# Mixer input products by seven block products for eight, and all mixers ahead of projections and heads

## The chip, the cores and the metric

The kernel runs on one core of a Trainium2 chip. TensorE (PE) multiplies matrices into PSUM, VectorE (DVE) and GpSimd (POOL) do arithmetic on whole tiles, ScalarE (ACT) applies functions and copies, and SyncE (SP) issues most DMAs. Each engine works through its own instructions in order and waits on semaphores for the others. The metric is the time of one execution in microseconds (us): the median of the runs, with lowest and highest.

## The reference

The trunk has two layers over 2048 positions of width 1024. Cut to what matters:

```python
def _short_conv_mixer(h, w_in, w_conv, w_out):
    u = h @ w_in                                   # 1024 -> 4 * 1024
    b_gate, c_gate, xin, g = jnp.split(u, 4, axis=-1)
    y = b_gate * _causal_depthwise_conv(c_gate * xin, w_conv)      # width 3
    return (y * jax.nn.silu(g)) @ w_out

# layer 0:  x = x + mixer(rmsnorm(x));  k, v = split(rmsnorm(x) @ w_kv), 8 heads of 64
# layer 1:  q, g = split(rmsnorm(x) @ w_in_b)
#           z = q k^T / 8, strictly causal;  w = exp(z + reverse_cumsum(log_sigmoid(-z)))
#           x = x + ((w @ v) * silu(g)) @ w_out_b
# output:   rmsnorm(x)
```

So the products with `w_in` are about half of the dense work of both layers together: 1024 x 4096 weights for every position.

## The kernel before

**Tiles.** Everything is held transposed: features on the 128 partitions, positions along the tile. Positions are reversed and cut into four chunks of 512 columns; chunk 0 holds the earliest. A width of 1024 is 8 blocks of 128 (`KD`). Every fp32 operand of a dense product is split into a high and a low fp32r part (`split`, lines 477 to 479: ACT makes the high part, DVE the low part as a difference), and `mm3` (line 501) adds three products, high x high, high x low, low x high, for each of the 8 steps of k: 24 matmuls of 128 x 128 by 128 x 512 for one output block.

**Mixers.** `mixer_in` (line 573) takes chunks 0 and 1 together as part `m01`: for each of 8 column blocks `cb` it loads and splits the four weights C, X, B and G once, stores the split form to DRAM (`load_w`, line 487), and multiplies them with both chunks. Chunks 2 and 3 follow as parts `m2` and `m3`, which read the split weights back. For chunks 0 and 1 the RMS norm is applied late, to the products (`late_rms`, line 540); for chunks 2 and 3 the sums of squares come from `stats_x` (line 550) and the norm is applied to x in `norm_x` (line 558). After the products come p = C * X, the convolution with a halo of two columns carried from chunk to chunk, and the gates B and silu(G); the result goes to DRAM as `y_d`.

**The rest.** `fold_gains` (line 643) multiplies the norm gains into the weights of the heads and stores their split form. `proj_out` (line 667, parts `po0` to `po3`) computes the output projection of a chunk, its residual and norm. `proj` (line 737, `p00` to `p33`) makes k, q and v of two heads, `proj_gate` (line 742, `g0` to `g3`) the gates. `attention` (line 752, `a00` to `a37`: chunk and head) goes over blocks of 512 keys from the latest to the first; for each of four groups of 128 queries it takes a sigmoid of the scores, a running product on DVE (`tensor_tensor_scan`), and a multiplication, then transposes the weights on PE, splits them and multiplies them with v. Only the block on the diagonal is shortened. `out_b`, `out_norm`, `out_b_last` and `finish` (lines 841 to 920) are the last projection and norm.

**Order.** Nothing is issued while these functions run. A recorder (lines 168 to 350) keeps every operation, gives it a key from the table `PLAN` (start and end per part, line 32), and `order` then builds each engine's fixed order: at each step it takes, of all operations whose inputs and tile buffers are free by a table of costs, the one that can start first, and of those the one with the lowest key. Buffers have tags with a number of turns (line 24: `whl` for split weights, `wraw` for raw weights, `act` for split activations, `og`, `ld`, `w`, `R`, ...); a tile must wait until an earlier tile of its tag is done with. All recorded instructions are emitted at line 350, which is why the profile names that line for nearly all of them, and tiles are told apart by their names: `pC`, `pX`, `pB`, `pG` are the mixer's input products, `po` the output projection, `pk`, `pq`, `pv`, `pg` the heads' products, `z`, `R`, `w`, `wt`, `wth`, `wtl`, `av` those of attention, `pob` and `pol` the last projection.

Of the kernel before, what the change touches and what calls it, by code (L numbers as in the profile page):

```python
# [10 lines left out]
F32 = mybir.dt.float32  # L11
# [5 lines left out]
P = 128  # L17
# [6 lines left out]
NR, NW, NT, NL, NWB, NRAW, NA, NWTS = 5, 8, 4, 5, 4, 2, 16, 2  # L24
# [143 lines left out]
class Recorder:  # L168
# [76 lines left out]
    def places(self, plan):  # L245
# [15 lines left out]
        for o in self.ops:  # L261
            o.left = len(o.deps)
            for d in o.deps:
                d.after.append(o)

        todo, n = [o for o in self.ops if not o.left], 0
        while n < len(todo):
            o = todo[n]
            n += 1
            for u in o.after:  # L270
                u.key = max(u.key, o.key)
                u.left -= 1
                if not u.left:
                    todo.append(u)
        rank = {id(o): k for k, o in enumerate(todo)}
        done = sorted(self.ops, key=lambda o: (o.key, rank[id(o)]))
# [82 lines left out]
def kernel(  # L359
# [121 lines left out]
    def w_tile(nm, kt=KD):  # L481
# [504 lines left out]
```

## Time and profile before

| | |
|---|---|
| median of 3 runs | 1809.22 us (1808.72 to 1812.49) |
| profiled execution, its own time | 1809.78 us |
| its span | 1808.1 us, granted TensorE clock 0.99 |
| HBM read and written | 326.92 MB and 136.05 MB |

The span runs from the first to the last instruction of the profiled execution. The profile gives for each engine its busy time, for each group of instructions its count and duration, and for each idle time the instruction that ended it. PE is an exception: matmuls overlap in its pipeline and their ends are modelled, so a matmul's listed mean (0.39 us) is longer than the distance between two of them.

### The profile page before, as it was taken

What the parts mean: (1) busy time and instruction counts of PE and PEld (TensorE: products, weight loads), DVE (VectorE), ACT (ScalarE), POOL (GpSimd) and SP (SyncE); (2) the same over time, 40 slices, a digit from 0 to 9 for tenths busy, and PEclk for the clock granted to TensorE, in tenths of its full rate; (3) what the DMA queues carried; (4) which work ended last, traced back from release to release, by engine and by line L of the source; (5) the groups of instructions that cost most, each with busy time, mean ns of one, the idle gap of its engine ahead of it and who ended that gap; (6) DMA issues with size and microseconds to landing.
All of it is one profiled execution on the core that took longest, in us unless ns stands there. A gap on an engine that the chain in (4) does not pass through costs nothing.

```text
span 1808.1 us, 24782 instructions
## 1 busy us (share of the span) xinstructions
PE 1755.3 (97%) x8312; PEld 1425.4 (79%) x8312; DVE 1234.5 (68%) x1830; ACT 777.2 (43%) x1493; POOL 418.5 (23%) x814
## 2 busy tenths in 40 slices
PE   7999999999999999999999999999999999999994
PEld 5788888887888888888878878888887888787762
DVE  6876644464244363558386749997468999999995
ACT  5433311232133232335243436665345666677652
POOL 5100000101021021112021312333112223346464
PEclk9999999999999999999999999999999999999996
DMA  9999955699878798668666576555878656879886
GB/s 298 331 352 352 363 200 162 202 306 352 289 272 273 239 352 267 240 218 302 216 228 230 184 249 206 181 185 185 273 241 313 210 193 221 277 240 322 265 285 206
DMA packets 234639, 464.63 MB, mean 257 GB/s; under 512 B 18704, under 2 KB 125200, under 8 KB 209936
## 3 DMA queue, kind: packets, MB, share of 16 engines
q1 hardware_dynamic: 174432, 404.28, 64.9%
q10 hardware_dynamic: 59920, 58.74, 11.2%
q8 instruction: 66, 1.08, 0.2%
q14 instruction: 61, 0.50, 0.1%
q0 software_dynamic: 160, 0.02, 0.1%
HBM read 326.92 MB, written 136.05 MB: 256 GB/s over the span
## 4 chain that ended last, share of the span: by engine, by line
PE 79%; DVE 9%; DMA 6%; issue 4%; ACT 1%; POOL 1%; SPq 0%; ACTq 0%; POOLq 0%; DVEq 0%
PE pB L350 9%; PE pG L350 9%; PE pC L350 9%; PE po L350 8%; PE pX L350 8%; PE av L350 6%; PE z L350 6%; PE wt L350 5%; PE pk L350 5%; PE pv L350 4%; PE pq L350 4%; PE pg L350 3%; PE pob L350 3%; DVE R L350 3%; DVE w L350 2%
## 5 line engine op out<-in xcount | busy, mean ns | idle before, releaser
L350 DVE TENSOR_TENSOR_SCAN R<-R,R,ones 128x512 f32<-128x512 f32 x192 | 250.4, 1313 | 15.3 <-ACT R L350 14.9
L350 ACT ACTIVATE R<-z 128x512 f32<-128x512 f32 (+2 forms) x320 | 173.6, 544 | 150.3 <-PE z L350 114.0
L350 ACT CAST wth<-wt 128x512 fp32r<-128x512 f32 (+2 forms) x320 | 156.1, 526 | 178.7 <-PE wt L350 146.2
L350 DVE TENSOR_TENSOR wtl<-wt,wth 128x512 fp32r<-128x512 f32 (+2 forms) x320 | 181.8, 598 | 64.9 <-ACT wth L350 61.4
L350 PE MATMUL pC<-h,whl_C 128*128 128x512 f32 x768 | 207.0, 399 | 8.3 <-ACT whl_C L350 8.0
L350 PE MATMUL z<-kt,q 128*128 128x512 f32 (+2 forms) x640 | 207.8, 387 | 1.8 <-DMA kt<-k_d 1.0
L350 PE MATMUL pB<-h,whl_B 128*128 128x512 f32 x768 | 208.3, 395 | 1.1 <-ACT whl_B L350 1.0
L350 PE MATMUL pG<-h,whl_G 128*128 128x512 f32 x768 | 207.1, 395 | 0.0
L350 PE MATMUL po<-y,whl_o 128*128 128x512 f32 x768 | 205.0, 394 | 0.5 <-ACT y L350 0.5
L350 DVE TENSOR_TENSOR w<-w,R 128x512 f32<-128x512 f32 (+2 forms) x320 | 201.3, 642 | 5.4 <-POOL R L350 0.5
L350 PE MATMUL pX<-h,whl_X 128*128 128x512 f32 x768 | 201.3, 396 | 0.4 <-ACT whl_X L350 0.4
L350 PE MATMUL wt<-ident,w 128*128 128x128 f32 x1088 | 195.9, 274 | 3.6 <-DVE w L350 3.4
L350 ACT ACTIVATE w<-z 128x512 f32<-128x512 f32 (+2 forms) x320 | 171.8, 544 | 49.9 <-PE z L350 48.0
L350 PEld LDWEIGHTS pC<-h,whl_C 128*128 128x128 f32 x768 | 143.1, 190 | 41.1 <-ACT whl_C L350 8.0
L350 PEld LDWEIGHTS wt<-ident,w 128*128 128x128 f32 x1088 | 139.6, 140 | 44.4 <-DVE w L350 10.9
L350 POOL COPY R<-R 128x1 f32<-128x1 f32 x192 | 93.5, 487 | 325.3 <-DVE R L350 273.5
L350 PEld LDWEIGHTS pX<-h,whl_X 128*128 128x128 f32 x768 | 142.6, 188 | 32.6 <-issue 1.9
L350 PEld LDWEIGHTS po<-y,whl_o 128*128 128x128 f32 x768 | 142.7, 188 | 31.6 <-ACT y L350 0.9
L350 PEld LDWEIGHTS pB<-h,whl_B 128*128 128x128 f32 x768 | 141.8, 188 | 29.9 <-ACT whl_B L350 1.5
L350 PEld LDWEIGHTS pG<-h,whl_G 128*128 128x128 f32 x768 | 142.4, 188 | 28.4
L350 DVE TENSOR_TENSOR_SCAN R<-R,ones 128x128 f32<-128x128 f32 (+3 forms) x128 | 112.2, 885 | 40.8 <-POOL R L350 39.4
L350 PEld LDWEIGHTS z<-kt,q 128*128 128x128 f32 x640 | 112.3, 189 | 20.4 <-ACT w L350 1.8
(152 smaller groups left out, 2593.2 us busy)
## 6 DMA issues: line engine op xcount, KB each, us to landing
whl_o<-sw_o SPq DMA_DIRECT2D x24, 1024.0 KB, 6.1
kt<-k_d ACTq DMA_DIRECT2D x80, 256.0 KB, 4.2
vv<-v_d ACTq DMA_DIRECT2D x80, 256.0 KB, 4.8
whl_C<-sw_C SPq DMA_DIRECT2D x16, 1024.0 KB, 6.0
whl_X<-sw_X SPq DMA_DIRECT2D x16, 1024.0 KB, 6.4
whl_k<-sw_kv SPq DMA_DIRECT2D x16, 1024.0 KB, 7.1
whl_B<-sw_B SPq DMA_DIRECT2D x16, 1024.0 KB, 6.7
whl_G<-sw_G SPq DMA_DIRECT2D x16, 1024.0 KB, 5.7
```

Of the source, the lines that this page charges most:

```text
L350: getattr(o.engine.engine, o.name)(*map(real, o.args), **{k: real(v) for k, v in o.kw.items()})
```

## The change

**Seven products for eight.** Two gates form a pair, (C, X) and (B, G). For one column block, the two gates times the two halves of the input width are a 2 x 2 table of weight blocks, A; the two halves of the input times two chunks are a 2 x 2 table of operands, B. Each block product has 4 steps of k instead of 8, so the plain way is 8 block products of 12 matmuls. `fast_unit` takes 7, with sums of weight blocks (`s1` to `s4`) and of operands (`t1` to `t4`), and accumulates parts of them in three PSUM banks (`fa`, `fd`, `fe`). ACT copies a bank at three points (`keep`), DVE adds a bank to a copy at three.

**What feeds it.** `fast_weights` loads four raw blocks, forms the seven weights and splits them; in the first pair of chunks it also stores them, and the second pair reads them back. Column blocks 0 and 1 of chunks 0 and 1 stay plain (`NPL = 2`), so the second pair forms those two again. `fast_first` and `fast_rest` (parts `x0`, `x1`) build the 7 x 4 operands of chunks 0 and 1 from x and the late norm, with their sums on POOL; `fast_all` (part `x2`) builds those of chunks 2 and 3, with the sums on DVE. There is one set of operand buffers, under tags that attention uses later (`HOMES`).

**Order.** `m2` and `m3` are replaced by one part for each pair of chunks and column block (`m02` to `m07`, `m20` to `m27`). `PLAN` is new in all its numbers. The tiles of the output projection (`act`) come after the operands of the second pair, so all mixers come ahead of it. `places` now takes keys in the order of recording. Split weights are held as tiles of 4 steps of k (`Q`), so the output projection and the heads load two tiles for one. Nothing else in projections and attention changes.

```diff
-NR, NW, NT, NL, NWB, NRAW, NA, NWTS = 5, 8, 4, 5, 4, 2, 16, 2
+NR, NW, NT, NL, NWB, NRAW, NA, NWTS = 5, 8, 4, 5, 8, 4, 16, 2
+
+Q, NPL = 4, 2
...
-    "m01": (-696.3, -373.1), "s2": (116.9, 307.1), "s3": (-527.4, -474.4), "fold": (141.2, 142.2),
...
+    "m01": (-29.9, 8.6), "x0": (-61.5, 68.4), "x1": (10.0, 14.7), "s2": (58.9, 306.1), "s3": (218.5, 388.6),
...
+    def w_tile(nm, kt=Q):
...
+        first = key not in split_d
+        if first:
+            split_d[key] = [dram.tile([P, 2, Q, P], F32, name=f"sw_{nm}_{j}") for j in range(0, kt, Q)]
+        wts = []
+        for j, d in enumerate(split_d[key]):
+            wt = w_tile(f"{nm}_{j}")
+            if first:
+                raw = sb.tile([P, Q, P], F32, name=f"wr_{nm}_{j}", tag="wraw", bufs=NRAW)
+                nc.sync.dma_start(out=raw, in_=src[j * Q * P:(j + 1) * Q * P, :].rearrange("(k p) n -> p k n", p=P))
+                split(wt[:, 0], wt[:, 1], raw, eng)
+                nc.sync.dma_start(out=d, in_=wt.bitcast(F32))
+            else:
+                nc.sync.dma_start(out=wt.bitcast(F32), in_=d)
+            wts.append(wt)
+        return wts
...
-            tag, bufs = (("w", NW), ("R", NR) if k < NR else ("ld", NL))[c]
+            tag, bufs = (("og", KD), ("ld", NL) if k < NL else ("vv", 2) if k == NL else ("ot", 2))[c]
...
-        if len(cs) == 1:
-            h[cs[0]] = norm_x(cs[0])
-        for cb in range(KD):
+
+        for cb in range(NPL):
...
+    HOMES = {"b11": ["w"] * 8, "t1": ["R"] * 5 + ["wth"] * 2 + ["wtl"], "t2": ["act"] * 4, "b22": ["act"] * 4,
+             "b21": ["act"] * 4, "t3": ["act"] * 4, "t4": ["q2", "q2", "kt", "kt", "vv", "vv"]}
+    BUFS = {"w": NW, "R": NR, "wth": NWTS, "wtl": NWTS, "act": NA, "q2": 2, "kt": 2, "vv": 2}
+    fast_b = {}
+    def operand(c, nm, k, raw):
+        if k == 0:
+            fast_b[c, nm] = []
+            home[nm] = list(HOMES[nm])
+        tag = home[nm].pop(0)
+        if tag in ("act", "q2"):
+            t = sb.tile([P, 2, CH], F32R, name=f"op_{nm}_{c}_{k}", tag=tag, bufs=BUFS[tag])
+            pair = (t[:, 0, :], t[:, 1, :])
+        else:
+            tags = [tag, home[nm].pop(0)]
+            pair = tuple(sb.tile([P, CH], F32R, name=f"op{m}_{nm}_{c}_{k}", tag=tg, bufs=BUFS[tg]) for m, tg in enumerate(tags))
+        split(pair[0], pair[1], raw)
+        fast_b[c, nm].append(pair)
+    home = {}
+    def fast_norm(x, k, r):
+        nc.vector.scalar_tensor_tensor(out=x, in0=x, scalar=gains["a"][:, k:k + 1], in1=r, op0=ALU.mult, op1=ALU.mult)
+    def fast_first(c):
+        x1, x2 = x_in[c + 1], x_in[c]
+        for k in range(Q):
+            fast_norm(x1[k], k, late[c + 1][0])
+            fast_norm(x2[k], k, late[c][0])
+            operand(c, "b11", k, x1[k])
+            nc.gpsimd.tensor_sub(x1[k], x2[k], x1[k])
+            operand(c, "t1", k, x1[k])
+        for k in range(Q):
+            fast_norm(x2[k + Q], k + Q, late[c][0])
+            fast_norm(x1[k + Q], k + Q, late[c + 1][0])
+            nc.gpsimd.tensor_sub(x1[k], x2[k + Q], x1[k])
+            nc.gpsimd.tensor_sub(x2[k], x2[k + Q], x2[k])
+    def fast_rest(c):
+        x1, x2 = x_in[c + 1], x_in[c]
+        for k in range(Q):
+            operand(c, "t2", k, x1[k])
+            operand(c, "b22", k, x2[k + Q])
+            operand(c, "b21", k, x1[k + Q])
+            operand(c, "t3", k, x2[k])
+            nc.gpsimd.tensor_sub(x1[k + Q], x1[k + Q], x1[k])
+            operand(c, "t4", k, x1[k + Q])
+    def fast_all(c):
+        rs = []
+        for i in (c, c + 1):
+            r = sb.tile([P, CH], F32, name=f"rs_{i}", tag="acc", bufs=2)
+            nc.scalar.copy(r, bcast(rx[i], f"hb{i}"))
+            rs.append(r)
+        for k in range(Q):
+            b = {}
+            for nm, i, kk in (("b11", 1, k), ("b12", 0, k), ("b22", 0, k + Q), ("b21", 1, k + Q)):
+                x = b[nm] = sb.tile([P, CH], F32, name=f"x{nm}_{c}_{k}", tag="og", bufs=KD)
+                nc.sync.dma_start(out=x, in_=xT[kk * P:(kk + 1) * P, cols(c + i)])
+                fast_norm(x, kk, rs[i])
+            operand(c, "b11", k, b["b11"])
+            nc.vector.tensor_sub(b["b11"], b["b12"], b["b11"])
+            operand(c, "t1", k, b["b11"])
+            nc.vector.tensor_sub(b["b11"], b["b22"], b["b11"])
+            operand(c, "t2", k, b["b11"])
+            nc.vector.tensor_sub(b["b12"], b["b22"], b["b12"])
+            operand(c, "b22", k, b["b22"])
+            operand(c, "b21", k, b["b21"])
+            operand(c, "t3", k, b["b12"])
+            nc.vector.tensor_sub(b["b21"], b["b21"], b["b11"])
+            operand(c, "t4", k, b["b21"])
+    NAMES = ("a11", "s1", "s2", "s4", "a12", "s3", "a22")
+    def fast_weights(c, cb, gs):
+        nm = f"{gs[0][0]}{cb}_{c}"
+        key = ("fast", gs[0][0], cb)
+        w = {}
+        if key in split_d:
+            for n in NAMES:
+                w[n] = w_tile(f"{n}_{nm}")
+                nc.sync.dma_start(out=w[n].bitcast(F32), in_=split_d[key][n])
+            return w
+        if c == 0:
+            split_d[key] = {n: dram.tile([P, 2, Q, P], F32, name=f"sw_{n}_{nm}") for n in NAMES}
+        a = {}
+        for n, (g, i), j in (("a11", gs[0], 0), ("a21", gs[1], 0), ("a22", gs[1], Q), ("a12", gs[0], Q)):
+            a[n] = sb.tile([P, Q, P], F32, name=f"fr_{n}_{nm}", tag="wraw", bufs=NRAW)
+            src = w_in_a[0][j * P:(j + Q) * P, i * D + cb * P: i * D + (cb + 1) * P]
+            nc.sync.dma_start(out=a[n], in_=src.rearrange("(k p) n -> p k n", p=P))
+        def sp(n, raw):
+            w[n] = w_tile(f"{n}_{nm}")
+            split(w[n][:, 0], w[n][:, 1], raw)
+            if c == 0:
+                nc.sync.dma_start(out=split_d[key][n], in_=w[n].bitcast(F32))
+        sp("a11", a["a11"])
+        sp("a22", a["a22"])
+        nc.vector.tensor_add(a["a22"], a["a21"], a["a22"])
+        sp("s1", a["a22"])
+        nc.vector.tensor_sub(a["a21"], a["a11"], a["a21"])
+        sp("s3", a["a21"])
+        nc.vector.tensor_sub(a["a11"], a["a22"], a["a11"])
+        sp("s2", a["a11"])
+        sp("a12", a["a12"])
+        nc.vector.tensor_sub(a["a12"], a["a12"], a["a11"])
+        sp("s4", a["a12"])
+        return w
+    def fast_unit(c, cb, gs, w):
+        nm = f"{gs[0][0]}{cb}_{c}"
+        def product(bank, wn, bn, start, stop):
+            n = 0
+            for k in range(Q):
+                for i, m in ((0, 0), (0, 1), (1, 0)):
+                    nc.tensor.matmul(bank, w[wn][:, i, k, :], fast_b[c, bn][k][m], start=start and n == 0,
+                                     stop=stop and n == 3 * Q - 1, skip_group_check=True)
+                    n += 1
+        def keep(n, ps):
+            t = ld512(f"{n}_{nm}")
+            nc.scalar.copy(t, ps)
+            return t
+        a = psum.tile([P, CH], F32, name=f"fa_{nm}", tag="lin", bufs=NLIN)
+        d = psum.tile([P, CH], F32, name=f"fd_{nm}", tag="z", bufs=NZ)
+        e = psum.tile([P, CH], F32, name=f"fe_{nm}", tag="wt", bufs=NWT)
+        product(a, "a11", "b11", True, False)
+        c11 = keep("f1", a)
+        product(d, "s1", "t1", True, False)
+        p5 = keep("f5", d)
+        product(a, "s2", "t2", False, False)
+        c12 = keep("f2", a)
+        product(d, "s4", "b22", False, True)
+        nc.vector.tensor_add(c12, c12, d)
+        product(e, "a12", "b21", True, True)
+        nc.vector.tensor_add(c11, c11, e)
+        product(a, "s3", "t3", False, False)
+        nc.vector.tensor_add(p5, p5, a)
+        product(a, "a22", "t4", False, True)
+        return ((c12, p5), (c11, a))
+    conv = {}
+    def fast_conv(cb, c, cc, x):
+        p = sb.tile([P, CH + 2], F32, name=f"p_{cb}_{c}", tag="p", bufs=2)
+        nc.vector.tensor_mul(p[:, 0:CH], x, cc)
+        nc.gpsimd.tensor_copy(p[:, CH:CH + 2], halo[:, cb, :])
+        nc.gpsimd.tensor_copy(halo[:, cb, :], p[:, 0:2])
+        t = conv[cb, c] = t512(f"cv_{cb}_{c}")
+        nc.scalar.activation(t, p[:, 0:CH], AF.Copy, scale=cw[:, 2, cb:cb + 1])
+        nc.vector.scalar_tensor_tensor(out=t, in0=p[:, 1:CH + 1], scalar=cw[:, 1, cb:cb + 1], in1=t,
+                                       op0=ALU.mult, op1=ALU.add)
+        nc.vector.scalar_tensor_tensor(out=t, in0=p[:, 2:CH + 2], scalar=cw[:, 0, cb:cb + 1], in1=t,
+                                       op0=ALU.mult, op1=ALU.add)
+    def fast_out(cb, c, b, g):
+        t = conv[cb, c]
+        nc.vector.tensor_mul(t, t, b)
+        sg = t512(f"sg_{cb}_{c}")
+        nc.scalar.activation(sg, g, AF.Sigmoid)
+        nc.vector.tensor_mul(t, t, sg)
+        nc.vector.tensor_mul(t, t, g)
+        nc.sync.dma_start(out=y_d[c][cb], in_=t)
+    def mixer_fast(c, cb):
+        for gs, use in (((("C", 1), ("X", 2)), fast_conv), ((("B", 0), ("G", 3)), fast_out)):
+            w = fast_weights(c, cb, gs)
+            for i, (first, second) in enumerate(fast_unit(c, cb, gs, w)):
+                use(cb, c + i, first, second)
...
+    part("x0", fast_first, 0)
+    part("x1", fast_rest, 0)
     for c in (2, 3):
         part(f"s{c}", stats_x, c)
     part("fold", fold_gains)
-    for c in (2, 3):
-        part(f"m{c}", mixer_in, (c,))
+    part("x2", fast_all, 2)
+    for c in (0, 2):
+        for cb in range(NPL if c == 0 else 0, KD):
+            part(f"m{c}{cb}", mixer_fast, c, cb)
```

More of the change, by code (lines that the diff above doesn't have):

```diff
@@ L261, in places @@
         for o in self.ops:
-            o.left = len(o.deps)
             for d in o.deps:
                 d.after.append(o)
[L266 to L276, printed above, removed]
+                assert d.index < o.index
+                o.key = max(o.key, d.key)
+        done = sorted(self.ops, key=lambda o: (o.key, o.index))
         for k, o in enumerate(done):
@@ L465, in rstd_bcast, with square_into @@
         return bcast(rstd(acc, nm), nm)
-    def square_into(acc, src, first, nm, eng=nc.vector, early=False):
+    def square_into(acc, src, first, nm, eng=nc.vector, home=("t", NT)):
         if first:
@@ L470, in square_into @@
         else:
-            tag = "wth" if early else "t"
-            sq = sb.tile([P, CH], F32, name=f"sq_{nm}", tag=tag, bufs=NT if tag == "t" else NWTS)
+            sq = sb.tile([P, CH], F32, name=f"sq_{nm}", tag=home[0], bufs=home[1])
             nc.scalar.activation(sq, src, AF.Square)
@@ L487, in load_w @@
     def load_w(src, key, nm, kt=KD, eng=nc.vector):
-        if key not in split_d:
-            wt = w_tile(nm, kt)
-            raw = sb.tile([P, kt, P], F32, name=f"wr_{nm}", tag="wraw", bufs=NRAW)
-            nc.sync.dma_start(out=raw, in_=src.rearrange("(k p) n -> p k n", p=P))
-            split(wt[:, 0], wt[:, 1], raw, eng)
-            split_d[key] = dram.tile([P, 2, kt, P], F32, name=f"sw_{nm}")
-            nc.sync.dma_start(out=split_d[key], in_=wt.bitcast(F32))
-            return wt
-        wt = w_tile(nm, kt)
-        nc.sync.dma_start(out=wt.bitcast(F32), in_=split_d[key])
-        return wt
+        first = key not in split_d
[13 more added lines that the diff above has]
+        return wts
     def mm3(ps, wts, a, kt=KD):
-        hi, lo = wts[:, 0], wts[:, 1]
         n = 0
         for k in range(kt):
-            for w, m in ((hi, 0), (hi, 1), (lo, 0)):
-                nc.tensor.matmul(ps, w[:, k, :], a[k][:, m, :], start=n == 0, stop=n == 3 * kt - 1)
+            for w, m in ((0, 0), (0, 1), (1, 0)):
+                nc.tensor.matmul(ps, wts[k // Q][:, w, k % Q, :], a[k][:, m, :], start=n == 0, stop=n == 3 * kt - 1)
                 n += 1
@@ L536, in squares @@
         for k, x in enumerate(xs):
-            square_into(acc, x, k == 0, f"h{c}{k}", nc.gpsimd, early=True)
+            square_into(acc, x, k == 0, f"h{c}{k}", nc.gpsimd, ("wth", NWTS))
         return acc
@@ L541, in late_rms @@
         pb = bcast(y, f"h{c}")
-        r = sb.tile([P, CH], F32, name=f"rs_{c}", tag="w", bufs=NW)
+        r = sb.tile([P, CH], F32, name=f"rs_{c}", tag=("kt", "wtl")[c], bufs=2)
         nc.scalar.copy(r, pb)
-        r2 = sb.tile([P, CH], F32, name=f"rs2_{c}", tag="w", bufs=NW)
+        r2 = sb.tile([P, CH], F32, name=f"rs2_{c}", tag=("kt", "vv")[c], bufs=2)
         nc.scalar.activation(r2, pb, AF.Square)
@@ L553, in stats_x @@
         for k in range(KD):
-            square_into(acc, load_x(c, k, "s"), k == 0, f"h{c}{k}", early=True)
+            square_into(acc, load_x(c, k, "s"), k == 0, f"h{c}{k}")
         y = const.tile([P, 4], F32, name=f"rx_{c}")
         rx[c] = rstd(acc, f"h{c}", y)
-    def norm_x(c):
-        hc = []
-        pb = bcast(rx[c], f"hb{c}")
-        for k in range(KD):
-            x = load_x(c, k, "n")
-            nc.vector.scalar_tensor_tensor(out=x, in0=x, scalar=gains["a"][:, k:k + 1], in1=pb,
-                                           op0=ALU.mult, op1=ALU.mult)
-            hc.append(act_tile(f"h_{c}", k))
-            split(hc[k][:, 0, :], hc[k][:, 1, :], x)
-        return hc
     h = {}
     turn = [0]
-    late_acc, late = {}, {}
+    late_acc, late, x_in = {}, {}, {}
     def mixer_in(cs):
-        if len(cs) == 1:
-            h[cs[0]] = norm_x(cs[0])
-        for cb in range(KD):
+        for cb in range(NPL):
             wts = {}
@@ L646, in fold_gains @@
             for i in range(KD):
-                split_d[nm, i] = dram.tile([P, 2, KD, P], F32, name=f"sw_{nm}{i}")
+                split_d[nm, i] = [dram.tile([P, 2, Q, P], F32, name=f"sw_{nm}{i}_{j}") for j in range(0, KD, Q)]
                 for j in range(0, KD, 4):
@@ L662, in fold_gains @@
             for m, t in enumerate((hi, lo)):
-                nc.sync.dma_start(out=split_d["ob", ob][:, m], in_=t.bitcast(F32))
+                nc.sync.dma_start(out=split_d["ob", ob][0][:, m], in_=t.bitcast(F32))
     kept = {}
@@ L875, in out_b_last @@
         for ob in range(KD):
-            wts = w_tile(f"ob{c}_{ob}", 3)
-            nc.sync.dma_start(out=wts.bitcast(F32), in_=split_d["ob", ob][:, :, 0:3, :])
+            wts = [w_tile(f"ob{c}_{ob}", 3)]
+            nc.sync.dma_start(out=wts[0].bitcast(F32), in_=split_d["ob", ob][0][:, :, 0:3, :])
             ps = lin(f"pob_{c}_{ob}")
@@ L883, in out_b_last @@
         for ob in range(KD):
-            nc.sync.dma_start(out=wl[ob // 4][:, :, ob % 4, :].bitcast(F32), in_=split_d["ob", ob][:, :, 3, :])
+            nc.sync.dma_start(out=wl[ob // 4][:, :, ob % 4, :].bitcast(F32), in_=split_d["ob", ob][0][:, :, 3, :])
         sg = sb.tile([P, CH], F32, name=f"sgl_{c}", tag="hl", bufs=1)
```

18 lines of the change are left out of this document (8 added, 10 removed), and 37 rows, old and new, of the table PLAN.

## The prediction

> **What bounds the kernel now.** I read the page's engine totals first, then the slices, then the chain that ended last.
>
> ```profile
> span 1808.1 us, 24782 instructions
> PE 1755.3 (97%) x8312; PEld 1425.4 (79%) x8312; DVE 1234.5 (68%) x1830; ACT 777.2 (43%) x1493; POOL 418.5 (23%) x814
> ...
> PE   7999999999999999999999999999999999999994
> ...
> DVE  6876644464244363558386749997468999999995
> ...
> PE 79%; DVE 9%; DMA 6%; issue 4%; ACT 1%; POOL 1%; SPq 0%; ACTq 0%; POOLq 0%; DVEq 0%
> ```
>
> TensorE (PE) has work in every slice and carries 79% of the chain: it is the bound. VectorE (DVE) averages 68%, but its slices go from 2 to 9; the 9s lie at the end. What a PE saving is worth therefore depends on whether DVE can still feed PE afterwards. The stretches, with the columns of the view in its first line:
>
> ```profile
> core 0: us, PE busy (x) PEld busy (x) DVE busy (x) ACT busy (x) POOL busy (x), PEclk, DMA share, GB/s
> 0.00:107.00 107.00, 95.66 (x404) 74.85 (x405) 79.17 (x121) 54.11 (x84) 30.09 (x39) 1.00 1.02 322
> ...
> 0.00:370.00 370.00, 358.65 (x1571) 292.83 (x1571) 221.06 (x324) 126.53 (x185) 43.59 (x66) 1.00 0.87 284
> 370.00:1400.00 1030.00, 1021.82 (x4885) 835.64 (x4885) 639.56 (x979) 400.87 (x823) 204.25 (x488) 1.00 0.74 252
> ...
> 1400.00:1500.00 100.00, 100.00 (x524) 81.88 (x522) 97.21 (x135) 67.27 (x135) 24.04 (x61) 1.00 0.61 201
> ...
> 1600.00:1700.00 100.00, 97.70 (x485) 77.11 (x484) 97.01 (x129) 71.05 (x137) 49.53 (x71) 1.00 0.85 288
> ...
> 1750.00:1808.10 58.10, 28.83 (x109) 19.18 (x107) 36.52 (x61) 14.60 (x25) 31.54 (x24) 0.74 0.68 219
> ```
>
> To see: up to 370 us the plain products of chunks 0 and 1 run with PE full and DVE at 60%. From 370 to 1400 the products of chunks 2 and 3 stand between the heads, and DVE is at 62%. From 1400 on DVE is at 97%, and PE still loses only 0 to 2.3 us in 100. In the last 58 us both run dry.
>
> **What the change removes.** The four groups of input products, and two of them in order of time (the first column is the start):
>
> ```profile
> L350 PE MATMUL pC<-h,whl_C 128*128 128x512 f32 x768 | 207.0, 399 | 8.3 <-ACT whl_C L350 8.0
> ...
> L350 PE MATMUL pB<-h,whl_B 128*128 128x512 f32 x768 | 208.3, 395 | 1.1 <-ACT whl_B L350 1.0
> L350 PE MATMUL pG<-h,whl_G 128*128 128x512 f32 x768 | 207.1, 395 | 0.0
> ...
> L350 PE MATMUL pX<-h,whl_X 128*128 128x512 f32 x768 | 201.3, 396 | 0.4 <-ACT whl_X L350 0.4
> ```
>
> ```profile
> 101.77 5.60 PE L350 MATMUL pG<-h,whl_G 128*128 128x512 f32 x24
> 107.21 5.60 PE L350 MATMUL pC<-h,whl_C 128*128 128x512 f32 x24
> ```
>
> 24 matmuls take 107.21 - 101.77 = 5.44 us, so one costs 0.2267 us. A unit (one gate pair, one column block, two chunks) had 4 x 24 = 96 of them and now has 7 x 12 = 84. Chunks 0 and 1 have 2 x 6 such units (column blocks 0 and 1 stay plain), chunks 2 and 3 have 2 x 8: 28 units x 12 = 336 matmuls, **76.2 us** of PE. Nothing else leaves PE; the output projection, heads and attention keep their counts.
>
> **What it adds.** None of it on PE; prices from these groups (count, busy, mean ns of one):
>
> ```profile
> L350 DVE SCALAR_TENSOR_TENSOR cv<-p,cw,cv 128x512 f32<-128x512 f32 x64 | 47.7, 745 | 11.1 <-ACT cv L350 9.5 <-POOL p L350 0.9
> ...
> L350 DVE TENSOR_TENSOR x<-x,po 128x512 f32<-128x512 f32 x32 | 21.9, 686 | 70.8 <-PE po L350 70.8
> ...
> L350 ACT COPY cs<-pC 128x512 f32<-128x512 f32 x32 | 18.8, 588 | 66.8 <-PE pC L350 63.9 <-DMA vv<-v_d 2.8
> ...
> L350 DVE SCALAR_TENSOR_TENSOR cv<-p,cw,cv 128x512 f32<-128x512 f32 x64 | 47.7, 745 | 11.1 <-ACT cv L350 9.5 <-POOL p L350 0.9
> ...
> L350 DVE SCALAR_TENSOR_TENSOR xn<-xn,g_a,prb_hb 128x512 f32<-128x512 f32 x16 | 11.3, 736 | 2.3 <-PE prb_hb L350 2.3
> ...
> L350 DVE TENSOR_TENSOR fold_kv<-fold_kv,fold_kv 128x512 fp32r<-128x512 f32 x16 | 11.0, 686 | 1.4 <-ACT fold_kv L350 1.1
> ```
>
> A unit lasts 84 x 0.2267 = 19.0 us. Beside it run three ACT copies of 0.59 (1.8 us) and three DVE adds of 0.69 (2.1 us). Where its seven weight forms are made (12 units of chunks 0 and 1, 4 of chunks 2 and 3) come 7 splits and 4 sums, 11 x 0.69 = 7.6 us of DVE. Per column block of two units in the first pair, DVE has 2 x (7.6 + 2.1) + 4.4 for the two convolutions (0.69 + 2 x 0.745 each) + 6 x 0.69 for the gates = 27.9 us in 38.1: hidden, with 10.2 us to spare. Without that cover each instruction would cost PE its 0.69. In the second pair DVE has less still, so folding the gains (72 instructions of 0.69 us, 50 us) goes under it. ACT's work is under half of the unit. DMA: a column block of the first pair reads 2.1 MB and stores 14 forms of 0.52 MB and 0.5 MB of gates, 10 MB; at the 322 GB/s of the first row above that is 31 us, under 38.1, so it costs nothing while the queue keeps its lead, and a gain has no reason.
>
> *Start of the first pair.* The normed x (16 x 0.736 = 11.8), the 28 splits (19.2) and the first unit's weights (7.6) are 38.6 us of new DVE work; in the first 107 us, about the length of the plain part, DVE idles 107 - 79.2 = 27.8. Excess 10.8. The 16 POOL subtractions take 16 x 1.41 = 22.6 us more, and how far DVE can work beside them shows here:
>
> ```profile
> 1754.23 2.19 POOL L350 TENSOR_TENSOR acc_x<-acc_x,sq_x 128x512 f32<-128x512 f32 x1
> 1756.37 1.72 POOL L350 TENSOR_TENSOR x2r<-x2r,pbs 128x512 f32<-128x512 f32 x1
> ```
>
> ```profile
> 1755.27 3.36 DVE L350 TENSOR_TENSOR w<-w,R 128x512 f32<-128x512 f32 x2
> ```
>
> Two DVE products took 3.36 us instead of 1.4 beside two POOL ones. Without any overlap the excess is 10.8 + 22.6 = 33.4. Bounds 0 (the last operands are made under the first units, which have 10.2 us to spare a column block) and 33.4; I take **20**, near the middle of 10.8 and 33.4. The Trainium skill, page "GPSIMD Engine Reference", section "Specifications", says that GpSimd's way into SBUF is shared with VectorE and that instructions with two SBUF inputs contend for it; the two rows agree, and by that rule alone this term would be 33 us and the time 1782.
>
> *From the first pair to the second.* The operands exist once, so the second pair's can be written only as the last unit lets go. 16 norms, 16 differences and 28 splits are 11.8 + 11.0 + 19.2 = 42 us of DVE, and eight x tiles hold two of the four steps of k. So about 21 us come after the last product, beside a first unit of 19.0 us whose first product wants all four steps. Nothing else can fill PE: the output projection's tiles wait for the same buffers. Bounds 0 and 21; I take **8**.
>
> *Inside a unit.* The seventh product adds onto the bank that DVE must first read after the sixth: at least 0.69 for the add and 5.60 - 5.44 = 0.16 for the matmul's end, 0.85 x 28 = 24 us bare. The next unit's first product has another bank and can stand in between; behind the add on DVE wait convolution and splits, for which nobody hurries. Bounds 0 and 24; I take **6**. The copies for products 3 and 4 have one product (2.72 us) for 0.59: nothing.
>
> *To the output projection:* its first tiles follow buffers that come free during the last unit; 0 to 5, I take **2**. Weights there now come in two loads of half the size: same bytes, nothing.
>
> **The sum**, against the profiled execution: 1808.1 - 76.2 + 20 + 8 + 6 + 2 = 1767.9 us of span. Outside the span lie 1809.78 - 1808.1 = 1.7 us, and that execution stands 0.6 above the median: **1769 us**.
>
> That takes for granted that heads and projections, now alone, keep the PE pace that they have with mixers between them. DVE's share of that part: 1234.5 - 221.1 (the row to 370) - 90 (chunks 2 and 3: 16 blocks of 0.69 + 2 x 0.745 + 3 x 0.69, and 23 for norm and splits) = 923 us; PE's is 1808 - 370 - 348 (1536 products) = 1090. 85% on the mean, where the rows from 1400 on show 97% with PE nearly full. So I let PE keep the lead.
>
> **The rivals.**
>
> *DVE becomes the bound after the mixers* (chance 0.20).
>
> ```profile
> L350 DVE TENSOR_TENSOR_SCAN R<-R,R,ones 128x512 f32<-128x512 f32 x192 | 250.4, 1313 | 15.3 <-ACT R L350 14.9
> ...
> L350 DVE TENSOR_TENSOR wtl<-wt,wth 128x512 fp32r<-128x512 f32 (+2 forms) x320 | 181.8, 598 | 64.9 <-ACT wth L350 61.4
> ...
> L350 DVE TENSOR_TENSOR w<-w,R 128x512 f32<-128x512 f32 (+2 forms) x320 | 201.3, 642 | 5.4 <-POOL R L350 0.5
> ```
>
> A full block of attention costs DVE 4 scans, 4 products and 4 splits, 4 x (1.31 + 0.64 + 0.60) = 10 us, and PE about half. DVE idles while two output projections and the first two heads' products are made (2 x 43.5 + 16.3 = 103 us of PE with some 74 DVE instructions of 0.69, 51 us: 52 idle), and 22 at the end: 923 / 0.97 + 52 + 22 = 1026, against PE's 1090. The 64 between them shrink as soon as late heads (two of DVE to one of PE) stand without projections beside them. If both limits bind through that part, PE loses 2.3 in 100 as in the row from 1600: 25 us, 1794. For it: heads and products no longer have 348 us of mixer products to stretch over. Against it: the gate and output projections may be held back for the last heads.
>
> *The units stall, slower than before* (0.10). The place is the hand-over from the sixth to the seventh product. If the add stands behind four DVE instructions and the next unit's product isn't put in between, each unit waits 0.85 + 4 x 0.69 = 3.6 us: 101 us instead of 6, 1864. It turns the sign from (1809 - 1763) / 28 = 1.6 us a unit, that is with one instruction ahead of the add. For it: DVE at 27.9 of 38.1 us and an order that is fixed beforehand. Against, two neighbours in order of time and the largest of PE's waits (us in total, times, longest):
>
> ```profile
> 443.55 0.39 PE L350 MATMUL pq<-xn,whl_q 128*128 128x512 f32 x1
> 443.77 0.62 PE L350 MATMUL pG<-h,whl_G 128*128 128x512 f32 x2
> ```
>
> ```profile
> PE prb_x L350 <- DVE dg_x L350: 9.9, 2, 6.6
> ```
>
> Products of two destinations alternate on PE at the same 0.22 us, and PE's waits on DVE are few.
>
> *The boundaries are covered* (0.15): the three stage ends and the hand-over cost 0 to 10 together: about 1738.
>
> That fewer matmuls are issued than the diff says is excluded by counting; that their time stays by the 0.2267 isn't.
>
> **How the numbers follow.** The forecast, 1750 to 1788, has 0.55. The range 1736 to 1806 takes in the covered case and the bound DVE, and leaves out the stalling units and the far ends of the start's and the pair change's bounds, 2 in 10. 0.2% (3.6 us) is what a measurement can tell. Faster: 0.55 + 0.15 + 0.16 of the first rival = 0.86. Same: 0.04, its far end. Slower: 0.10.
>
> **What would show it.** 2736 input matmuls, 24 in 5.44 us as before; PE gaps near 110, between the pairs, and at the output projection of some 20, 8 and 2 us; PE waits on the DVE adds below 0.3 us a unit; the last product of the mixers near 680 us; after it DVE above 85% and PE above 97%. It is wrong if PE idles in the later part beside a DVE at 97%, or if waits inside units sum to over 20 us.

## The result, and the profile after

| | before | changed |
|---|---|---|
| median of 4 runs | 1810.63 us (1808.72 to 1812.49) | 1759.95 us (1751.64 to 1762.25) |
| ratio | | 0.9712 [0.9677, 0.9747] |
| profiled execution, its own time | 1809.78 us | 1762.25 us |
| its span | 1808.1 us | 1760.4 us |

The change makes the kernel 2.9% faster (2.5 to 3.2%). That is 51 us between the medians, and 47.7 us between the spans. The runs of the changed kernel spread over 10.6 us, against 3.8 before; a difference of a few us between two variants of it therefore says little, and below I compare the ratios to the kernel before, each with its interval.

The page of the changed kernel: totals (busy time, share, count), slices of PE and DVE, and the shares of the chain that ended last.

```profile
span 1760.4 us, 25320 instructions
...
PE 1693.4 (96%) x7976; PEld 1369.1 (78%) x7976; DVE 1391.8 (79%) x2118; ACT 875.3 (50%) x1695; POOL 474.2 (27%) x830
...
PE   7999999999999999999999999999999999999975
...
DVE  6988777997546355433388999999999999999996
...
PE 74%; DVE 11%; DMA 7%; issue 3%; ACT 2%; POOL 1%; ACTq 0%; POOLq 0%; SPq 0%; DVEq 0%
```

PE has 8312 - 7976 = 336 matmuls less, as counted from the diff. DVE has 157 us more. Its low slices now lie together from 440 to 880 us (slices 11 to 20), under the second pair of the mixers and the first output projections; from slice 23 (968 us) it stands at 9 up to the last but one. The stretches of the changed kernel, columns as in the prediction's view:

```profile
core 0: us, PE busy (x) PEld busy (x) DVE busy (x) ACT busy (x) POOL busy (x), PEclk, DMA share, GB/s
...
104.40:140.00 35.60, 32.60 (x133) 25.62 (x132) 29.47 (x46) 16.82 (x32) 9.28 (x8) 0.95 0.77 258
...
104.40:341.70 237.30, 234.30 (x1017) 190.23 (x1016) 191.30 (x315) 102.80 (x178) 20.42 (x29) 0.99 0.82 280
...
341.70:371.00 29.30, 26.80 (x109) 19.62 (x108) 29.06 (x48) 14.00 (x24) 1.33 (x2) 1.00 0.71 235
...
371.00:662.00 291.00, 288.28 (x1256) 234.92 (x1255) 171.21 (x262) 90.67 (x154) 10.86 (x36) 1.00 0.87 289
...
662.00:900.00 238.00, 231.97 (x1044) 188.82 (x1043) 105.47 (x180) 69.47 (x136) 34.26 (x65) 0.99 0.96 336
...
900.00:1700.00 800.00, 780.58 (x4010) 635.23 (x4008) 766.21 (x1129) 526.64 (x1087) 328.65 (x630) 0.99 0.76 243
...
1700.00:1760.40 60.40, 36.42 (x144) 25.09 (x144) 43.59 (x64) 17.48 (x31) 31.87 (x25) 0.81 0.54 174
```

And the boundaries in order of time on PE (start, duration, tile, count; in brackets the wait ahead of it):

```profile
98.94 5.60 PE L345 MATMUL pG<-h,whl_G 128*128 128x512 f32 x24
104.38 2.96 PE L345 MATMUL fa_C<-op_b,whl_a_C 128*128 128x512 f32 x12
...
122.61 1.22 PE L345 MATMUL fd_C<-op_b,whl_s_C 128*128 128x512 f32 x2 [2.19 <-DVE op_b L345]
...
657.54 1.52 PE L345 MATMUL po<-y,whl_o 128*128 128x512 f32 x6
659.34 3.05 PE L345 MATMUL fa_B<-op_t,whl_a_B 128*128 128x512 f32 x12 [0.28 <-DVE f_B L345]
662.22 43.92 PE L345 MATMUL po<-y,whl_o 128*128 128x512 f32 x193
```

What is to be seen. Matmuls keep their price: 24 in 104.38 - 98.94 = 5.44 us, 0.2267 each. The mixers end at 662.2, where the forecast had 680. Within a stretch of matmuls with 512 columns, its length less 0.2267 times the count is what PE lost there, to waits or to a lower granted clock, also where the busy column hides it (16 matmuls of the first pair have one column and are cheaper; with them its loss is up to 2 us larger than listed):

| stretch | matmuls x 0.2267 | lost |
|---|---|---|
| 104.4 to 341.7, first pair | 230.6 | 6.7 |
| of it 104.4 to 140, its start | 30.2 | 5.4 |
| 341.7 to 371, change of pairs | 24.7 | 4.6 |
| 371 to 662, rest of the second pair | 284.7 | 6.3 |

The three stages lose 6.7 + 4.6 + 6.3 = 17.6 us. In the start the granted clock is 0.95, which over 35.6 us makes 1.8 of the 5.4. The plain part ahead of it ends at 104.38 us, against 107.21 in the kernel before. After 662.0 the rest lasts 1760.4 - 662.0 = 1098.4 us, where the prediction had 1808 - 370 - 348 = 1090. The excess is in PE's idle time: 6.0 + 19.4 + 24.0 = 49.4 us from 662 on (last three rows), against 1438.1 - (1755.3 - 358.7) = 41.5 us from 370 on before. In 900 to 1700 PE loses 2.4 in 100 beside a DVE at 96%.

### The profile page after: what moved, and what is told of

Read it like the earlier page. It is cut to its first block, busy times and chain, and to the rows that moved or that the text cites. A ratio compares the mean times of both kernels' runs of the same rounds, so it can differ in the third digit from the quotient of the medians.

```text
span 1760.4 us, 25320 instructions
## 1 busy us (share of the span) xinstructions
PE 1693.4 (96%) x7976; PEld 1369.1 (78%) x7976; DVE 1391.8 (79%) x2118; ACT 875.3 (50%) x1695; POOL 474.2 (27%) x830
## 4 chain that ended last, share of the span: by engine, by line
PE 74%; DVE 11%; DMA 7%; issue 3%; ACT 2%; POOL 1%; ACTq 0%; POOLq 0%; SPq 0%; DVEq 0%
PE po L345 9%; PE fa_C L345 8%; PE fa_B L345 7%; PE av L345 6%; PE z L345 6%; PE wt L345 5%; PE pg L345 4%; PE pq L345 4%; PE pv L345 4%; PE pk L345 4%; PE fd_C L345 4%; PE pob L345 3%; PE fd_B L345 3%; PE fe_C L345 2%; DVE R L345 2%
## 5 line engine op out<-in xcount | busy, mean ns | idle before, releaser
L345 PE MATMUL wt<-ident,w 128*128 128x128 f32 x1088 | 186.0, 273 | 7.0 <-DVE w L345 4.5
L345 POOL COPY halo<-p 128x2 f32<-128x2 f32 x32 | 17.1, 534 | 477.8 <-DVE p L345 477.8
L345 DVE TENSOR_TENSOR_SCAN R<-R,ones 128x512 f32<-128x512 f32 (+3 forms) x128 | 111.1, 881 | 24.8 <-POOL R L345 24.3
L345 PE MATMUL av<-wtl,vv 128*128 128x512 f32 (+1 forms) x320 | 125.4, 395 | 1.7 <-DVE wtl L345 1.5
L345 PE MATMUL av<-wth,vv 128*128 128x512 f32 (+1 forms) x320 | 119.8, 374 | 1.8 <-DVE ot L345 0.8
L345 POOL TENSOR_SCALAR_AFFINE_SELECT R<-R 128x128 f32<-128x128 f32 x128 | 78.0, 612 | 141.7 <-ACT R L345 138.7
L345 PE MATMUL pob<-og,whl_ob 128*128 128x512 f32 x360 | 108.4, 411 | 5.3 <-DVE x1o L345 1.9
L345 PE MATMUL pk<-xn,whl_k 128*128 128x512 f32 x384 | 108.6, 405 | 3.2 <-ACT xn L345 1.2
L345 PE MATMUL pq<-xn,whl_q 128*128 128x512 f32 x384 | 111.2, 401 | 0.0
L345 PE MATMUL pv<-xn,whl_v 128*128 128x512 f32 x384 | 107.7, 398 | 0.0
```

Source lines behind the costliest of these rows:

```text
L345: getattr(o.engine.engine, o.name)(*map(real, o.args), **{k: real(v) for k, v in o.kw.items()})
```

## The experiments

Each time has its ratio to the kernel before, run beside it on the same chip. Four places were in question: whether the 76 us of matmuls came in full, what the new start cost, whether the hand-over inside a unit costs, and what holds the part behind the mixers.

### The eighth product put back

One product of each unit is issued twice into the same bank, so that PE has its 336 matmuls again while operands, boundaries and the keys in `PLAN` stay as in the change (`order` plans anew with the doubled product). The second starts the bank anew, so the value is the same.

```diff
         product(e, "a12", "b21", True, True)
+        product(e, "a12", "b21", True, True)
```

> The changed kernel with the product a12 x b21 of every unit issued twice, so that a unit has again 8 block products: 28 x 12 = 336 matmuls more, same result, same plan. Theory (the mixers are bound by TensorE, every matmul taken out counts in full): 76 us more than the changed kernel, 1836 us, a ratio of 1.014 to before; then order, operands and boundaries alone cost 26 us and the seven products give 76. Rival (a unit is paced by VectorE, ScalarE or the hand-overs): 40 us more or less, about 1800.

Measured: 1834.35 us (1830.16 to 1837.96), ratio 1.0138 [1.0109, 1.0167]. Its page:

```profile
span 1831.2 us, 25979 instructions
...
PE 1764.6 (96%) x8312; PEld 1429.3 (78%) x8312; DVE 1397.7 (76%) x2118; ACT 875.3 (48%) x1695; POOL 476.1 (26%) x830
```

And the end of its mixers on PE, in order of time:

```profile
733.65 2.96 PE L345 MATMUL fa_B<-op_t,whl_a_B 128*128 128x512 f32 x12
```

The last mixer product starts 733.65 - 659.34 = 74.3 us later than in the changed kernel, and the medians lie 74 us apart (77 by the ratios). The rest of the span, from that start on, is 1097.6 against 1101.1 us. The start of the first pair:

```profile
104.40:140.00 35.60, 32.61 (x141) 25.75 (x140) 30.84 (x46) 16.88 (x31) 9.70 (x6) 1.00 0.81 274
```

PE is busy there as long as in the changed kernel, but at a granted clock of 1.00, and loses 35.6 - 141 x 0.2267 = 3.6 us, 1.8 less. The medians show that the matmuls' time counts in full, and that all the rest of the change (operands, boundaries, order) costs 26 us net: 1834.35 against 1808.53 for the kernel before in the same session.

### Less work in the part behind the mixers

Three runs take work out of attention without a new plan: `order` still sees every operation, and the dropped ones are just not emitted. The first leaves out the product of the weights with the running product for one of the four query groups, 58 us of DVE. The second leaves out the matmul with the low part of q in the scores (the second of two; the first then closes the bank), 64 us of PE. The third leaves out both.

```diff
                 nc.vector.tensor_mul(w[:, lo:CH], w[:, lo:CH], R[:, lo:CH])
+                nc.ops[-1].drop = qi == 0
...
-            getattr(o.engine.engine, o.name)(*map(real, o.args), **{k: real(v) for k, v in o.kw.items()})
+            if not o.drop:
+                getattr(o.engine.engine, o.name)(*map(real, o.args), **{k: real(v) for k, v in o.kw.items()})
```

> The changed kernel in the same order of instructions, without the multiplication of the weights with the running product for the first of four query groups in every block of attention: 80 VectorE instructions of about 0.72 us, 58 us, are left out of the later part (the attention output is another). Theory A (TensorE bounds the later part): under 10 us less, 1750 or more. Theory B (VectorE bounds it from 900 us on): 40 to 55 us less, 1705 to 1720.

```diff
                 nc.tensor.matmul(ps[:, lom:CH], q2[:, 0, qi * P:(qi + 1) * P], kt[:, lom:CH], start=True, stop=False)
+                nc.ops[-1].kw["stop"] = True
                 nc.tensor.matmul(ps[:, lom:CH], q2[:, 1, qi * P:(qi + 1) * P], kt[:, lom:CH], start=False, stop=True)
+                nc.ops[-1].drop = True
```

> The changed kernel in the same order, without the second (low part) score product in every block of attention: 320 matmuls, 64 us of TensorE, are left out of the later part (scores lose the low part of q). Theory A (TensorE bounds the later part): 50 to 64 us less, about 1700. Theory B (VectorE bounds it from 900 us on): under 15 us less, 1745 or more. If each of this run and the one with less VectorE work gives 20 to 30 us, both bind in turn.

The third has both edits.

> The changed kernel with both cuts at once, 58 us of VectorE and 64 us of TensorE out of attention, in the same order of instructions. The single cuts gave 4 and 15 us. Theory D (both engines are at their limit in the same stretches, each cut alone left the other): 45 to 60 us less, 1700 to 1715. Theory O (what holds the time is the chain through the engines in an order that is fixed, not the load of either): 20 to 30 us less, 1730 to 1740.

| left out | us | ratio | against the change, by ratio |
|---|---|---|---|
| 58 us of DVE | 1756.11 | 0.9712 [0.9682, 0.9742] | 0 |
| 64 us of PE | 1744.50 | 0.9641 [0.9618, 0.9664] | -13 |
| both | 1723.85 | 0.9542 [0.9512, 0.9572] | -31 |

The same stretch in each of the three, in the order of the table. Without 58 us of DVE:

```profile
900.00:1700.00 800.00, 780.66 (x4021) 637.24 (x4020) 731.64 (x1062) 524.70 (x1085) 293.59 (x631) 0.99 0.77 244
```

Without 64 us of PE:

```profile
900.00:1700.00 800.00, 764.05 (x3749) 573.14 (x3747) 778.92 (x1142) 529.24 (x1090) 357.25 (x632) 0.99 0.77 246
```

Without both:

```profile
900.00:1700.00 800.00, 763.97 (x3807) 591.77 (x3806) 750.35 (x1085) 533.64 (x1105) 323.25 (x639) 0.99 0.78 250
```

Taking DVE work away lowers DVE from 766 to 732 of 800 us and PE goes no faster: 780.7 us and 4021 matmuls in the stretch, after 780.6 and 4010. Taking PE work away raises DVE to 779. The DVE cut that is worth nothing by itself is worth 18 us on top of the PE cut (0.9641 to 0.9542, intervals apart). So neither engine alone binds this part. Where the cuts go is seen in the waits of the same stretch (us in total, times, longest). The changed kernel:

```profile
DVE wtl L345 <- ACT wth L345: 10.0, 20, 1.7
...
PE av L345 <- DVE wtl L345: 1.5, 4, 0.9
...
PE wt L345 <- DVE w L345: 1.0, 3, 0.4
```

Without 58 us of DVE:

```profile
DVE wtl L346 <- ACT wth L346: 33.3, 56, 1.7
```

Without 64 us of PE:

```profile
PE wt L346 <- DVE w L346: 8.2, 14, 2.5
...
PE av L346 <- DVE wtl L346: 6.8, 11, 1.3
```

DVE's idle time grows by 34.6 us with the cut on DVE, and 23 of them are waits for the split that ACT makes of PE's transposed weights. PE's grows by 16.5 us with the cut on PE, and 12.5 of them are these two waits for DVE. So with the order of each engine fixed, much of a cut on one is turned into waits for the other. The result of both cuts, 31 us by the ratios and 36 by the medians, is in neither of the two ranges expected of it but between them.

### The same cuts in the kernel before

The first two cuts again, with the same edits, on the kernel before:

> The kernel before with the same 80 VectorE multiplications of attention left out, in the same order of instructions. Theory (TensorE bounds it, VectorE has room): no change, 1803 to 1811. Rival (VectorE bounds it from 1400 us on): 15 to 25 us less.

> The kernel before with the same 320 low score products (64 us of TensorE) left out, in the same order. Theory (TensorE alone bounds it up to 1400 us, where about 390 of the 640 score products stand, and VectorE stands at its limit behind): some 35 to 50 us less, 1760 to 1775; so the kernel before had VectorE time to spare that the changed one has not. Rival (before and after stand alike): 13 us less as with the changed kernel, 1795.

Measured: without the DVE work 1805.72 us over 10 runs, 0.9991 [0.9979, 1.0002], no change; without the PE work 1795.18 us, 0.9928 [0.9908, 0.9949]. I had taken the kernel before to be bound by PE up to 1400 us, where DVE idles 38%, so most of the 64 us should have come back. 13 did, as many as in the changed kernel. The same 100 us of the kernel before:

```profile
700.00:800.00 100.00, 100.00 (x485) 82.14 (x484) 48.72 (x74) 33.14 (x70) 15.99 (x40) 1.00 0.69 235
```

and of the one without the matmuls:

```profile
700.00:800.00 100.00, 99.36 (x470) 79.28 (x469) 48.94 (x73) 33.66 (x71) 15.85 (x40) 1.00 0.71 240
```

15 matmuls fewer, DVE at 49% in both, the same progress by DVE's and ACT's counts, and PE is still busy for 99.36 us of 100. A full busy column is therefore no proof that PE is the limit: the listed ends of matmuls reach past the start of the next (0.39 us listed at a distance of 0.2267), and they cover short waits. Without the matmuls, the weight loads of the stretch wait in three places where those of the kernel before don't (us in total, times, longest):

```profile
PEld av L351 <- DVE wtl L351: 1.2, 5, 0.3
...
PEld av L351 <- ACT wth L351: 1.0, 3, 0.4
...
PEld wt L351 <- DVE w L351: 0.8, 2, 0.5
```

PEld's busy time follows the count: 82.1 to 79.3 is 3.5% less, beside 3.1% fewer matmuls. The Trainium skill, page "Trainium Kernel Development and Optimization", section "Performance Expectations", calls matmul busy time a bad metric for the distance from the peak, because matmuls are pipelined, and names the busy share of the weight loads as a good one; the two rows of the stretch agree.

### The cuts with a new plan

The two kernels without the second score matmul once more, with its cost set to zero for the planner as well, so that `order` arranges the rest anew:

```diff
+                nc.ops[-1].drop = True
+                nc.ops[-1].busy, nc.ops[-1].late = 0.0, 0.0
```

> The changed kernel without the 320 low score products as before (64 us of TensorE), but the planner knows that they cost nothing and orders everything anew. Theory B (VectorE binds the later part): no more than with the old order, 1735 to 1750. Theory O (the old order kept the time): 1700 to 1720.

> The kernel before without the 320 low score products, the planner knowing that they cost nothing. With the old order they gave 13 us of 64. Theory (the kernel before has VectorE time to spare up to 1400 us, and only the old order kept the time): 35 to 60 us less, 1750 to 1775. Rival (VectorE's late stretch or the chain of attention holds it): 15 us less as before, 1795.

Measured: 1768.68 us, 0.9779 [0.9748, 0.981], on the changed kernel, and 1801.2 us, 0.9961 [0.9946, 0.9976], on the one before. Both are slower than with the old order (1744.5 and 1795.18), and the first is slower than with the matmuls in. Neither time lies in a range expected of it. The keys in `PLAN` were set for other costs. The pair shows how much the order is worth (24 us here for the same instructions), not how much a plan made for these cuts would gain; that stays open.

### The start: subtractions off GpSimd

The 16 subtractions of `fast_first` and `fast_rest` move to DVE, so that GpSimd and DVE hardly work side by side any more.

```diff
-            nc.gpsimd.tensor_sub(x1[k], x2[k], x1[k])
+            nc.vector.tensor_sub(x1[k], x2[k], x1[k])
...
```

> The changed kernel with the 16 differences of the first pair's operands on VectorE instead of GpSimd. Theory of the collision (22.6 us of GpSimd stand in VectorE's way): the gaps between 104 and 140 us, 5 us, go or shrink; 1755 to 1760. Rival (GpSimd takes work off a VectorE that is full there): 11 us more on VectorE before the first units, gaps of 5 to 15 us more, 1765 to 1775. Third case (all of it is under the plain products): no change.

Five subtractions of the changed kernel in order of time on GpSimd, which the prediction had at 1.41 us each:

```profile
108.55 1.29 POOL L345 TENSOR_TENSOR xh<-xh,xh 128x512 f32<-128x512 f32 x1 [6.96 <-DVE op_b L345]
115.53 4.67 POOL L345 TENSOR_TENSOR xh<-xh,xh 128x512 f32<-128x512 f32 x2 [5.69 <-DVE op_b L345]
126.92 2.87 POOL L345 TENSOR_TENSOR xh<-xh,xh 128x512 f32<-128x512 f32 x2 [6.72 <-DVE op_b L345]
```

and three DVE instructions beside them:

```profile
108.92 1.47 DVE L345 TENSOR_TENSOR whl_s_C<-fr_a_C,whl_s_C 128x512 fp32r<-128x512 f32 x1
...
119.63 1.12 DVE L345 TENSOR_TENSOR op_t<-xh,op_t 128x512 fp32r<-128x512 f32 x1 [1.84 <-ACT op_t L345]
...
129.04 0.69 DVE L345 TENSOR_TENSOR f_C<-f_C,fe_C 128x512 f32<-128x512 f32 x1 [1.66 <-PE fe_C L345]
```

The kernel with the subtractions on DVE, its totals:

```profile
PE 1690.6 (97%) x7976; PEld 1367.3 (78%) x7976; DVE 1391.4 (80%) x2134; ACT 874.0 (50%) x1695; POOL 451.9 (26%) x814
```

its stretch at the start of the first pair:

```profile
104.40:140.00 35.60, 35.60 (x157) 29.15 (x156) 33.22 (x55) 18.89 (x33) 1.93 (x4) 1.00 0.86 279
```

and the end of its mixers in order of time:

```profile
652.73 3.05 PE L345 MATMUL fa_B<-op_t,whl_a_B 128*128 128x512 f32 x12 [1.09 <-DVE f_B L345]
```

157 matmuls in place of 133: the 5.4 us are gone, though DVE got work on top, and the mixers' last product starts 6.6 us earlier. The granted clock is 1.00 there in place of 0.95. The place of the loss is shown, and that it goes when these 16 instructions leave GpSimd (`order` plans anew around them); how much of it is their own length (in all 26.4 us on GpSimd, 10.7 on DVE), how much the mutual slowing and how much the clock isn't told apart. DVE's busy total is the same (1391.8 and 1391.4) although it took on 10.7 us, so beside GpSimd's subtractions it had lost about as much. In the whole it is 1753.68 us (1752.06 to 1756.29), 0.9698 [0.967, 0.9726], whose interval overlaps the change's. The contention that the Trainium skill's page "GPSIMD Engine Reference", section "Specifications", names, and on which the prediction drew, is there. The DVE instruction at 108.92 took 1.47 us instead of 0.69 and ended 0.55 us after the subtraction beside it, as if it had waited for it. The pair at 115.53 took 4.67 us instead of 2.8 while DVE worked back to back up to 117.80; the next pair took 2.87, and there DVE stood idle for 1.66 us. The 33 us didn't come, PE lost 5.4. These rows don't speak against the two excluding each other; what failed is that all of GpSimd's time was put in PE's way.

### The start: less plain work in front of it

Only column block 0 stays plain, and block 1 joins the seven products, planned behind the next block (`m09`): 2 units, 24 matmuls or 5.4 us of PE less. With the keys (62.6, 62.7) for it `order` finds no operation that can go on, so that placing has no time.

```diff
-Q, NPL = 4, 2
+Q, NPL = 4, 1
...
+    "m09": (81.0, 106.0), ...
...
+            part("m09" if (c, cb) == (0, 1) else f"m{c}{cb}", mixer_fast, c, cb)
```

> The changed kernel with one plain column block in the first pair instead of two, the block that moves planned behind the next one: 24 matmuls or 5.4 us of TensorE less, 43.5 us of plain products less to cover the first pair's operands. Theory (the start cost little because the plain products covered it): TensorE gaps behind the plain part grow by 15 to 40 us, 1765 to 1795. Rival (the work at the start is small whatever stands over it): 5 us less, 1754.

Measured: 1777.53 us (1773.61 to 1781.8), 0.9831 [0.9809, 0.9854]. A stretch at its start:

```profile
60.00:100.00 40.00, 23.49 (x66) 14.00 (x67) 39.47 (x45) 18.20 (x32) 21.87 (x14) 0.83 0.34 116
```

the same stretch of the changed kernel:

```profile
60.00:100.00 40.00, 40.00 (x176) 32.80 (x175) 37.12 (x50) 18.01 (x30) 18.24 (x16) 1.00 0.34 124
```

and the end of the mixers of this run in order of time:

```profile
675.17 2.94 PE L345 MATMUL fa_B<-op_t,whl_a_B 128*128 128x512 f32 x12
```

With 5.4 us less for PE the mixers' last product starts 15.8 us later: 21 us lost. DVE is busy for 39.47 of 40 us, PE for 23.49 instead of 40. The operands' cost that I had forecast at the start is real; the second plain column block hides it. Some of the 21 us is the clock: granted 0.83 in these 40 us against 1.00, 6.8 us. Whether the gaps on PE bring the lower clock with them, no run here takes apart.

### The hand-over inside a unit

The seventh product adds onto the bank that DVE reads after the sixth. Here another product stands between the two:

```diff
-        product(e, "a12", "b21", True, True)
-        nc.vector.tensor_add(c11, c11, e)
         product(a, "s3", "t3", False, False)
         nc.vector.tensor_add(p5, p5, a)
+        product(e, "a12", "b21", True, True)
+        nc.vector.tensor_add(c11, c11, e)
```

> The changed kernel with the sixth and fifth product of a unit swapped, so that the product with a bank of its own (a12 x b21) stands between VectorE's read of the first bank and the seventh product. Theory (the next unit's first product already covers that read; the trace shows 2.7 us of waits there in all): no change, 1755 to 1762. Rival (the hand-over costs the 6 us that were forecast, or more): 1748 to 1754.

Measured: 1760.07 us, 0.9734 [0.9706, 0.9763]: no change. There was nothing to gain: PE's waits for that add in the changed kernel (us in total, times, longest) and the largest others inside the mixers are

```profile
PE fa_B L345 <- DVE f_B L345: 2.7, 3, 1.6
...
PE fd_C L345 <- DVE op_b L345: 2.2, 1, 2.2
PE fa_C L345 <- ACT f_C L345: 1.7, 2, 1.1
```

3 waits in 28 units. Where the next unit's product or an output projection stands in between, the add is in time.

### The fastest version found

The subtractions on DVE as above, and in `proj_out` also GpSimd's splits of the normed x for chunk 0:

```diff
-            split(xn[:, 0, :], xn[:, 1, :], x1[k], nc.gpsimd if k in XNL else nc.vector)
+            split(xn[:, 0, :], xn[:, 1, :], x1[k], nc.gpsimd if k in XNL and c else nc.vector)
```

> The changed kernel with the 16 differences of the first pair's operands on VectorE, as in the run that measured 1753.7, and with chunk 0's normed tiles all split on VectorE, which is at a third of its time there, instead of three of eight on GpSimd. If both gaps are what GpSimd's two-input work costs: 5 us less than the changed kernel at the start and 1 to 3 us less between 706 and 723 us, 1751 to 1754, a ratio of 0.968 to 0.970. If the first gain was scatter: 1757 to 1762.

Measured over 5 rounds: 1753.81 us (1747.74 to 1754.69), 0.9686 [0.9666, 0.9705]. Products behind the first output projection in the changed kernel, in order of time, and the stretch around them:

```profile
715.25 2.51 PE L345 MATMUL pk<-xn,whl_k 128*128 128x512 f32 x6 [0.85 <-POOL xn L345]
```

```profile
700.00:730.00 30.00, 26.39 (x106) 19.32 (x105) 17.28 (x33) 8.28 (x14) 4.38 (x3) 0.94 0.88 303
```

and the same stretch in this one:

```profile
700.00:730.00 30.00, 26.89 (x112) 20.48 (x111) 15.41 (x32) 7.01 (x12) 0.00 (x0) 1.00 0.91 324
```

GpSimd is out of it, and PE makes 6 matmuls more, about 1.4 us. But the granted clock is 1.00 there in place of 0.94, which over 30 us is 1.8 us, so it isn't shown that the splits gave the 6. By its ratio this kernel is the best with the whole computation in, level with the one with the subtractions alone on DVE (1753.68 us, 0.9698). Its interval still overlaps that of the change, so I don't call it faster than the change.

## Why the prediction was right, point by point

The direction and the size held: 1769 forecast, 1759.95 measured, 9 us below and within the forecast's own 1750 to 1788. But two errors partly cancel, so that it came this near is in part luck: the mixers came out 18 us shorter than forecast (14 to 16 in the three terms, 2.8 in the plain part, for which there was no term), the rest about 10 longer (1098.4 against 1767.9 - 680 = 1088).

- **336 matmuls, 76.2 us.** Right. Put back, they cost 74 us.
- **Start of the first pair, 20.** Measured 5.4, of which 1.8 is the lower clock: the term that was mis-sized most. The excess of DVE work and the collision with GpSimd are there, but I set DVE's work against its idle time in the plain part and let most of the excess stand in PE's way, where it could follow under the first units (the lower bound, 0, was nearer). With one plain block less, PE loses 21 us more, some 7 of it by the clock; with two, 5.4 are left, and they go when the subtractions leave GpSimd.
- **Change of pairs, 8.** Measured 4.6: DVE is busy for 29.06 of 29.3 us there, as argued.
- **Hand-over in a unit, 6.** The waits on DVE's add sum to 2.7 us, 0.1 a unit. All of the second pair behind its start loses 6.3, the first pair behind its own 6.7 - 5.4 = 1.3 (up to 3.3 with the 16 short matmuls). The case of stalling units is refuted: it needed 1.6 us in every unit to turn the sign, and that is the longest of three such waits.
- **To the output projection, 2.** The last wait is 0.28.
- **Heads and projections keep PE's pace, 0.** Off by 8. DVE's 923 us were nearly right (105.5 + 766.2 + 43.6 = 915 from 662 on), and PE's share from 662 to 1700 is (231.97 + 780.58) / 1038 = 97.5%, as the sign asked. DVE's share of the whole part is 83%, below the 85% named: 44% up to 900 and 96% from there on.
- **DVE becomes the bound, the first rival.** Half right. From 900 on the picture is the one it drew, DVE at 96% and PE losing 2.4 in 100; the sign of being wrong, PE idle beside a DVE at 97%, is all but met there. The price was too high, since the kernel before lost 41.5 us from 370 on as well, and the mechanism is another: 58 us of DVE work taken out gave nothing that can be told from zero.
- **Boundaries covered, 0 to 10.** The boundaries and the hand-over cost 5.4 + 4.6 + 2.7 + 0.3 = 13, between this case and the forecast.

A premise was wrong that the sum did not depend on: that PE "has work in every slice" and is the bound in the heads' part. The runs without score matmuls show that PE's time there comes back only for a fifth (13 of 64 us). In the mixers, long rows of independent matmuls, it comes back in full. Why the later part lost 8 us isn't settled: the runs show that PE and DVE hold each other there in a fixed order, but not which of the waits carries the 8.

## What to carry to other kernels

A matmul saved is worth its distance to the next only where PE runs rows of products that wait for nobody; so price a saving by the stretch, and test a claim that PE binds by leaving matmuls out, not by its busy share. New operand work ahead of a fast stage needs independent matmuls beside it, and it pays to leave a part of the stage in its old form for that. Operands that the next matmul waits for are better not made on GpSimd beside a busy DVE.

## What the hardware showed that I had not expected

PE's listed busy time stays at 99% in a stretch with 3% fewer matmuls and no faster progress. GpSimd's subtractions depend on what DVE does beside them: a pair took 4.67 us beside a DVE at work, the next 2.87 where DVE stood idle for 1.66. Taking 16 of them off GpSimd gave PE 5.4 us back, though DVE had more to do. In two runs the granted clock is lower where PE has gaps at the start, 0.95 in the changed kernel and 0.83 with one plain block less; with the eighth product the gaps there go with 1.00. Last, the same instructions in two orders differ by 24 us (1744.5 and 1768.68).
